# A 31-tap convolution on the tensor engine: from 64-column groups fed by on-chip shifted copies to 32-column groups fed by copies read back from device memory

## The chip, the cores and the metric

The kernel runs on all 8 cores of one Trainium2 chip, one program on each core and no exchange between them. The metric is the device time of the slowest core, in microseconds (us). The runs show two states: in some executions the cores of one die show a lower granted tensor clock and the run is some per cent longer. In one run of the kernel before (1240.1 us) cores 4 to 7 took 1188 to 1239 us at a clock of 0.87 to 0.91, and cores 0 to 3 took 1169 to 1175 us at 0.94 to 0.95. A median with its range is of all runs of a kernel, slow ones too; the ratio to before, with its 95% interval, is of the fast runs alone.

## The reference

One layer of a hybrid decoder trunk is applied to eight prompts of 2048 tokens and 128 short samples of 8 tokens. Each core takes one prompt and 16 samples: 2048 + 128 = 2176 tokens. The part that matters is branch B, a 31-tap depthwise convolution over tokens, per channel:

```python
u = _rmsnorm(h, g_mix)
proj = jnp.einsum('ntd,de->nte', u, w_in)              # D_MODEL = 1024, nine slices of 1024
a_b, a_c, a_h, a_z, b_v, b_g, b_z, gate_a, gate_b = jnp.split(proj, SPLITS, axis=-1)
...
v = b_v * jax.nn.sigmoid(b_g)                          # (N, T, 1024)
ext_b = jnp.concatenate([buf_b.astype(v.dtype), v], axis=1)   # 30 rows of history in front
c = _causal_dwconv(ext_b, w_conv_b) + b_conv_b         # 31 taps, each channel for itself
yb = jax.nn.silu(_layernorm(c, ln_g, ln_b)) * jax.nn.silu(b_z)
...
m = jax.nn.sigmoid(gate_a) * ya + jax.nn.sigmoid(gate_b) * yb
h = h + jnp.einsum('ntd,de->nte', m, w_o)
```

## The kernel before

Tokens are worked off in three blocks (768, 768, and 512 prompt tokens with 128 sample tokens), channels in eight chunks of 128. Operations are not issued as they are written down. They are added to a list (`Sched.add`) with the names of what they read and write, and waits are derived from the names: a read waits for the last writer, a write waits for the last writer and for all readers since.

```python
def add(self, eng, fn, reads=(), writes=(), dma=None):
    ...
    for r in reads:
        w = self.last_writer.get(r)
        if w is not None:
            deps.add(w)
            raw.add(w)
    for r in writes:
        w = self.last_writer.get(r)
        if w is not None:
            deps.add(w)
        for rd in self.readers.get(r, {}).values():
            deps.add(rd)
```

The convolution is a matmul. A group of 64 channels sits on 64 rows of the array, and a copy of it, shifted by one token, on the other 64 rows. So one matmul with a 128x64 diagonal weight does two taps, and 16 of them, each over data shifted by two more tokens, do all taps. Two groups of 64 columns make up a chunk. The shifted copies `R` are made by DMA from on-chip memory to on-chip memory, four loads for each piece of 512, 256 or 128 tokens, into buffers of their own:

```python
for g in range(2):
    for jj in range(2):
        ...
        S.add("sp", lambda e, src=src, dst=dst: e.dma_start(out=dst, in_=src),
              reads=rr, writes=[f"R{rs}_{g}_{jj}"], dma=f"R{rs}_{g}_{jj}")
...
for i in range(16):
    for g in range(2):
        ...
        S.add("pe", lambda e, ...: e.matmul(
            ps[64 * g:64 * g + 64, bc, 0:n], lhsT=Wp[ds][:, 16 * g + i, :], rhs=rhs,
            start=(i == 0), stop=(i == 15), tile_position=(0, 64 * g)), ...)
```

Of the kernel before, what the change touches and what calls it, by code (L numbers as in the profile page):

```python
# [13 lines left out]
KB = 31  # L14
# [5 lines left out]
V_GMIX, V_GPLE, V_BCONV, V_LNG, V_LNB = 0, 8, 16, 24, 32  # L20
V_WCA = 40
V_WCB = 64
V_MASK = V_WCB + 256
NV = V_MASK + 64

BLOCKS = [
    dict(p0=0, npr=768, sbs=[(0, 512, "p"), (512, 256, "p")]),
    dict(p0=768, npr=768, sbs=[(0, 512, "p"), (512, 256, "p")]),
    dict(p0=1536, npr=512, sbs=[(0, 512, "p"), (512, 128, "s")]),
]  # L30

class Sched:
    def __init__(self, nc):
        self.nc = nc
        self.ops = []
        self.last_writer = {}
        self.readers = {}
        self.chan_count = {}

    def add(self, eng, fn, reads=(), writes=(), dma=None):  # L40
        idx = len(self.ops)
        chan = eng if dma is None else ("dma", dma)
        deps = set()
        raw = set()
        for r in reads:
            w = self.last_writer.get(r)
            if w is not None:
                deps.add(w)
                raw.add(w)
# [94 lines left out]

def build_program():
# [9 lines left out]
    p_d = din("p", [NTOK, 256])  # L155
    sa_d = din("sa", [32, D])
    sb_d = din("sb", [480, D])
    w_in = din("w_in", [9 * NCH, 128, D])
    w_oa = din("w_oa", [NCH, 128, D])
    w_ob = din("w_ob", [NCH, 128, D])  # L160
    w_o = din("w_o", [D, D])
# [7 lines left out]
    ncap_d = dout("nca_p", [2, D])  # L169
    ncbp_d = dout("ncb_p", [30, D])  # L170
    ncas_d = dout("nca_s", [32, D])
    ncbs_new_d = dout("ncb_s_new", [128, D])
    ncbs_hist_d = dout("ncb_s_hist", [352, D])

    with contextlib.ExitStack() as st:
# [3 lines left out]
        idf = sb("idf", [128, 128], F32)  # L179
# [5 lines left out]
        histb = sb("histb", [128, NCH, 480], BF16)  # L185
        hista = sb("hista", [128, NCH, 32], F32)
        halo_v = sb("halo_v", [128, NCH, 30], BF16)
# [5 lines left out]
        NRING = 8  # L193
        ring = [sb(f"ring{i}", [128, NCH, 128], BF16) for i in range(NRING)]
# [3 lines left out]
        Wp = [sb(f"Wp{i}", [128, 32, 64], BF16) for i in range(2)]  # L198
        RL = 608
        NRS = 3  # L200
        Rb = [[sb(f"R{i}_{g}", [128, RL], BF16) for g in range(2)] for i in range(NRS)]
        vext = [sb(f"vext{i}", [128, 30 + NTB + 2], BF16) for i in range(2)]
        vexts = [sb(f"vexts{i}", [128, 624], BF16) for i in range(2)]
        sext = [sb(f"sext{i}", [128, 2 + NTB], F32) for i in range(1)]
        sexts = [sb(f"sexts{i}", [128, 160], F32) for i in range(1)]
        xs = [sb(f"xs{i}", [128, D], F32) for i in range(3)]
        xb = [sb(f"xb{i}", [128, D], BF16) for i in range(2)]
        ssq = sb("ssq", [128, 64], F32)
        msq = sb("msq", [128, 64], F32)
        rsd = sb("rsd", [128, 64], F32)  # L210
        NTMP = 6
        tmp = [sb(f"tmp{i}", [128, 512], F32) for i in range(NTMP)]
        accs = sb("accs", [128, NTB], F32)
        accq = sb("accq", [128, NTB], F32)
        rstdB = sb("rstdB", [128, NTB], F32)
        nmrB = sb("nmrB", [128, NTB], F32)
        Abuf = [sb(f"Abuf{i}", [128, D], F32) for i in range(2)]
        Bbuf = sb("Bbuf", [128, D], F32)
        yt = sb("yt", [128, D], F32)
        u2T = sb("u2T", [128, NCH, 128], BF16)  # L220
        pbt = [sb(f"pbt{i}", [128, 256], BF16) for i in range(2)]
        pT = sb("pT", [128, 2, 128], BF16)
        vkeep = sb("vkeep", [128, NCH, 32], F32)
        skeep = sb("skeep", [128, NCH, 2], F32)
        vkeep_s = sb("vkeep_s", [128, NCH, 128], F32)
        BB = [Bbuf[:, :], vkeep_s.rearrange("p a b -> p (a b)")]
        skeep_s = sb("skeep_s", [128, NCH, 32], F32)
# [3 lines left out]
        S = Sched(nc)  # L231

        free_banks = list(range(8))

        def balloc():
            return free_banks.pop(0)

        def bfree(b):
            free_banks.append(b)
# [3 lines left out]
        def talloc():  # L243
            k = tmp_ctr[0] % NTMP
            tmp_ctr[0] += 1
            return k

        ring_ctr = [0]

        SWQ = 4  # L250
        swq_ctr = [0]

        def swq():
            r = f"swq{swq_ctr[0] % SWQ}"
            swq_ctr[0] += 1
            return r

        WL, WG = [], []

        def add_group(srcs):  # L260
            WG.append(list(range(len(WL), len(WL) + len(srcs))))
            for sap in srcs:
                WL.append((sap, len(WG) - 1))
# [4 lines left out]
        for _bi in range(len(BLOCKS)):  # L268
            for j in range(NCH):
                add_group([wcol(4, j), wcol(5, j)])  # L270
            for j in range(NCH):
                add_group([wcol(1, j), wcol(2, j), wcol(0, j), wcol(3, j)])
                if j >= 4:
                    add_group([wcol(6, 2 * (j - 4))])
                    add_group([wcol(6, 2 * (j - 4) + 1)])
            for j in range(NCH):
                add_group([w_oa[j, :, :], w_ob[j, :, :], wcol(7, j), wcol(8, j)])
        wst = dict(nl=0, ng=0, done=set())

        def pump(maxn=4):  # L280
            nem = 0
            while nem < maxn and wst["nl"] < len(WL) and (wst["nl"] < NRING or WL[wst["nl"] - NRING][1] in wst["done"]):
                nem += 1
                t = wst["nl"]
                wst["nl"] += 1
                k = t % NRING
                src = WL[t][0]
                S.add("pool", lambda e, k=k, src=src: e.dma_start(  # L288
                    out=ring[k][:, :, :].rearrange("p k m -> p (k m)"), in_=src),
                    writes=[f"ring{k}", swq()], dma=f"ring{k}")  # L290

        def wgroup():
            g = wst["ng"]
            wst["ng"] += 1
            if not all(t < wst["nl"] for t in WG[g]):
                pump(NRING)
            assert all(t < wst["nl"] for t in WG[g]), "weight tile not prefetched"
            return g, [t % NRING for t in WG[g]]

        def wdone(g):  # L300
            wst["done"].add(g)
            pump()
# [3 lines left out]
        def rms_stats(src_ap, src_res, junk_ap, junk_res):  # L306
            c = stat_ctr[0] % 64
            stat_ctr[0] += 1
            S.add("act", lambda e, c=c: e.activation(out=junk_ap, in_=src_ap, func=AF.Square,
                                                     accum_out=ssq[:, c:c + 1]),  # L310
                  reads=src_res, writes=list(junk_res) + [f"ssq{c}"])
# [9 lines left out]
        def vcol(off, j):  # L321
            return vecs[:, off + j:off + j + 1]

        S.add("sp", lambda e: e.dma_start(out=idf[:], in_=ident_d), writes=["idf"], dma="idf")
        S.add("sp", lambda e: e.dma_start(out=vecs[:], in_=vecs_d), writes=["vecs"], dma="vecs")
        S.add("sp", lambda e: e.dma_start(out=gfin[:], in_=gfin_d), writes=["gfin"], dma="gfin")
        S.add("dve", lambda e: e.tensor_copy(out=idb[:], in_=idf[:]), reads=["idf"], writes=["idb"])
        S.add("pool", lambda e: e.memset(onesf[:], 1.0), writes=["onesf"])
        for i in range(2):
# [119 lines left out]
        for bi, blk in enumerate(BLOCKS):  # L449
# [34 lines left out]
            def s2_proj(j, si):  # L484
                off, n, kind = sbs[si]
                if si == 0:
# [4 lines left out]
                    if j < 2:  # L491
                        diag_build(j)
# [540 lines left out]
```

## Time and profile before

| | before |
|---|---|
| time, median of 3 runs (lowest, highest) | 1180.0 us (1179.0, 1286.6) |
| tensor engine (PE) busy | 1000.9 us, 85% of the span |
| mean granted tensor clock | 0.95 |
| convolution matmuls | 132 us (the two column groups run at once: 32 matmuls of 512 columns in 3.57 us, a pair per 223 ns) |
| waits of the convolution for its copies | 8.7 + 7.5 = about 16 us in all |
| packets on the hardware DMA queue (q1) | 24017, 43.4 MB |

The highest run is slow. PE is TensorE, DVE is VectorE, ACT is ScalarE, SP is the engine whose instruction queue issues the plain DMA loads. "SPq" in a line is that queue at work.

The page of the kernel before says first what is busy (busy us, share of the span, number of instructions):

```profile
PE 1000.9 (85%) x6774; PEld 562.7 (48%) x6774; DVE 560.9 (48%) x927; ACT 356.5 (30%) x661; POOL 231.0 (20%) x512
```

The chain of work that ended last, by engine and by line (a share of the span each):

```profile
PE 64%; DVE 11%; issue 9%; ACT 7%; DMA 7%; SPq 1%; DVEq 0%; POOL 0%; ACTq 0%; POOLq 0%
PE ps L687 13%; PE ps L571 10%; PE ps L790 10%; PE ps L508 9%; PE ps L891 6%; PE ps L779 5%; PE ps L784 5%; PE ps L643 3%; PE ps L844 3%; DMA t_xs<-x 2%; DMA t_R_1<-t_vext 2%; ACT t_tmp L661 2%; DVE t_cbuf L663 2%; DVE t_tmp L653 2%; DVE t_tmp L650 1%
```

The two groups of the convolution, L571, from the costliest groups (busy us, mean ns of one, then idle time just before them and what ended it):

```profile
L571 PE MATMUL ps<-t_R_0,t_Wp 128*64 128x512 bf16 (+2 forms) x768 | 132.5, 326 | 8.7 <-DMA t_R_0<-t_vext 8.7
L571 PE MATMUL ps<-t_R_1,t_Wp 128*64 128x512 bf16 (+2 forms) x768 | 131.7, 326 | 7.5 <-DMA t_R_1<-t_vext 7.5
```

The middle block by stage, from busy time in windows (start:end, length, then busy us and instructions of PE, PEld, DVE, ACT and POOL, then granted clock, DMA share, GB/s): projection with long convolution; short branch, LayerNorm and z gate; output and merge; final token tiles.

```profile
451.00:549.00 98.00, 95.16 (x772) 55.20 (x770) 43.64 (x57) 25.44 (x48) 12.27 (x33) 0.96 0.47 95
549.00:676.00 127.00, 111.34 (x670) 65.09 (x667) 79.94 (x154) 36.35 (x69) 25.94 (x57) 0.96 0.55 85
676.00:758.00 82.00, 81.67 (x498) 49.10 (x499) 26.84 (x50) 17.36 (x34) 16.04 (x31) 0.98 0.59 91
758.00:838.00 80.00, 59.78 (x318) 28.57 (x315) 42.79 (x49) 39.55 (x64) 18.99 (x42) 0.89 0.38 109
```

In the first of them the tensor engine has almost no gap: 95 of 98 us. And the timeline of the SP queue in that stage (start, length, what was issued, how often) shows how the copies are fed: two loads are issued in about 1.1 us.

```profile
469.73 1.19 SPq L542 DMA_DIRECT2D t_R_1<-t_vext  x2
473.60 1.10 SPq L542 DMA_DIRECT2D t_R_0<-t_vext  x2
474.86 1.53 SPq L542 DMA_DIRECT2D t_R_1<-t_vext  x2
```

### The profile page before, as it was taken

The numbers are of one execution on the slowest core, as the hardware profiler recorded it, in microseconds if no ns is written. First come the engines' busy times: TensorE is split into PE (matmuls) and PEld (weight loads), VectorE is DVE, ScalarE is ACT, GpSimd is POOL, SyncE is SP. The second block draws the span as 40 slices with busy tenths as digits, with TensorE's granted clock in tenths as the row PEclk, the third lists the DMA queues.
The fourth block names the chain that finished last, engine by engine and source line by source line (L and its number), as shares of the span: only waits on it lengthen the run. The fifth ranks groups of instructions, "written<-read, shape, count | busy, mean of one in ns | idle before, by whom it ended". The sixth has DMA issues, their size and how long they took to land.

```text
span 1178.2 us, 20798 instructions; the slowest of 8 cores (1166.8 to 1178.2 us)
## 1 busy us (share of the span) xinstructions
PE 1000.9 (85%) x6774; PEld 562.7 (48%) x6774; DVE 560.9 (48%) x927; ACT 356.5 (30%) x661; POOL 231.0 (20%) x512
## 2 busy tenths in 40 slices
PE   1689978988998856999989799987599978789884
PEld 0355645544654423555545465533355544445442
DVE  1334426655333563554566533346555556633353
ACT  3222323233112452223232321245323222332233
POOL 3120102212112121111122121212132222212111
PEclk9899989998999987999998999989799999989997
DMA  9695676554676233546455556633356546576221
GB/s 202 116 155 92 125 165 92 78 84 67 101 107 110 77 127 76 91 90 132 72 90 90 77 77 104 108 94 120 94 108 123 97 76 108 82 152 111 55 79 63
DMA packets 66971, 119.74 MB, mean 102 GB/s; under 512 B 8657, under 2 KB 23377, under 8 KB 66833
## 3 DMA queue, kind: packets, MB, share of 16 engines
q0 software_dynamic: 42848, 75.06, 42.1%
q1 hardware_dynamic: 24017, 43.36, 12.2%
q8 instruction: 56, 0.92, 0.3%
q14 instruction: 50, 0.41, 0.1%
HBM read 172.23 MB, written 11.14 MB: 156 GB/s over the span
## 4 chain that ended last, share of the span: by engine, by line
PE 64%; DVE 11%; issue 9%; ACT 7%; DMA 7%; SPq 1%; DVEq 0%; POOL 0%; ACTq 0%; POOLq 0%
PE ps L687 13%; PE ps L571 10%; PE ps L790 10%; PE ps L508 9%; PE ps L891 6%; PE ps L779 5%; PE ps L784 5%; PE ps L643 3%; PE ps L844 3%; DMA t_xs<-x 2%; DMA t_R_1<-t_vext 2%; ACT t_tmp L661 2%; DVE t_cbuf L663 2%; DVE t_tmp L653 2%; DVE t_tmp L650 1%
## 5 line engine op out<-in xcount | busy, mean ns | idle before, releaser
L687 PE MATMUL ps<-t_uT,t_ring 128*128 128x512 bf16 (+2 forms) x1536 | 254.6, 328 | 40.8 <-ACT t_tmp L661 22.1
L687 PEld LDWEIGHTS ps<-t_uT,t_ring 128*128 128x128 bf16 x1536 | 143.9, 101 | 150.1 <-issue 53.1
L288 POOL DMA_DIRECT2D t_ring<-w_in x216 | 115.7, 536 | 479.4 <-PE ps L508 213.8
L571 PE MATMUL ps<-t_R_0,t_Wp 128*64 128x512 bf16 (+2 forms) x768 | 132.5, 326 | 8.7 <-DMA t_R_0<-t_vext 8.7
L571 PE MATMUL ps<-t_R_1,t_Wp 128*64 128x512 bf16 (+2 forms) x768 | 131.7, 326 | 7.5 <-DMA t_R_1<-t_vext 7.5
L508 PE MATMUL ps<-t_uT,t_ring 128*128 128x512 bf16 (+2 forms) x768 | 130.3, 325 | 0.3 <-DVE t_uT L426 0.3
L790 PE MATMUL ps<-t_uT,t_ring 128*128 128x512 bf16 (+2 forms) x768 | 128.9, 322 | 0.0
L571 PEld LDWEIGHTS ps<-t_R_0,t_Wp 128*64 128x64 bf16 x768 | 75.8, 111 | 53.2 <-issue 21.1
L891 PE MATMUL ps<-t_wpg_t,t_u2T 128*128 128x512 bf16 x272 | 73.5, 432 | 31.5 <-DVE t_u2T L867 22.5
L508 PEld LDWEIGHTS ps<-t_uT,t_ring 128*128 128x128 bf16 x768 | 68.3, 99 | 59.2 <-issue 18.8
L790 PEld LDWEIGHTS ps<-t_uT,t_ring 128*128 128x128 bf16 x768 | 70.9, 99 | 50.5 <-issue 4.4
L801 DVE TENSOR_TENSOR t_tmp<-ps,t_tmp 128x512 f32<-128x512 f32 (+2 forms) x48 | 25.7, 535 | 123.7 <-ACT t_tmp L797 123.7
L571 PEld LDWEIGHTS ps<-t_R_1,t_Wp 128*64 128x64 bf16 x768 | 75.9, 111 | 15.1 <-issue 13.3
L784 PE MATMUL ps<-t_cbuf,t_ring 128*128 128x512 bf16 (+2 forms) x384 | 67.8, 319 | 8.9 <-DVE t_cbuf L663 8.9
L779 PE MATMUL ps<-t_yaT,t_ring 128*128 128x512 bf16 (+2 forms) x384 | 68.5, 322 | 6.3 <-ACT t_tmp L661 4.9
L657 ACT ACTIVATE t_tmp<-t_tmp,t_vecs 128x512 f32<-128x512 f32 (+2 forms) x48 | 33.0, 688 | 121.4 <-DVE t_tmp L653 121.4
L797 ACT ACTIVATE t_tmp<-ps 128x512 f32<-128x512 f32 (+2 forms) x48 | 22.7, 473 | 143.1 <-PE ps L790 142.3
L891 PEld LDWEIGHTS ps<-t_wpg_t,t_u2T 128*128 128x128 bf16 x272 | 28.5, 108 | 74.1 <-issue 52.5
L578 ACT ACTIVATE t_cbuf<-ps,t_vecs 128x512 f32<-128x512 f32 (+2 forms) x48 | 27.0, 563 | 119.6 <-PE ps L571 119.6
L422 PE MATMUL ps<-t_idb,t_xb 128*128 128x128 bf16 x136 | 15.6, 285 | 56.0 <-ACT t_xb L417 56.0
L844 PE MATMUL ps<-t_wo_t,t_cbuf 128*128 128x512 bf16 x272 | 61.0, 379 | 0.0
L643 PE MATMUL ps<-t_uT,t_ring 128*128 128x512 bf16 (+2 forms) x384 | 60.9, 317 | 0.0
(121 smaller groups left out, 1206.0 us busy)
## 6 DMA issues: line engine op xcount, KB each, us to landing
t_ring<-w_in POOLq DMA_DIRECT2D x216, 256.0 KB, 5.6
t_xs<-x SPq DMA_DIRECT2D x34, 512.0 KB, 4.2
y<-t_yt SPq DMA_DIRECT2D x17, 512.0 KB, 2.6
t_ring<-w_oa POOLq DMA_DIRECT2D x24, 256.0 KB, 4.2
t_ring<-w_ob POOLq DMA_DIRECT2D x24, 256.0 KB, 5.3
t_R_0<-t_vext SPq DMA_DIRECT2D x48, 67.8 KB, 2.0
t_R_1<-t_vext SPq DMA_DIRECT2D x48, 67.8 KB, 2.0
t_wo_t<-w_o POOLq DMA_DIRECT2D x2, 1024.0 KB, 10.3
```

The source lines that it names most:

```text
L288: S.add("pool", lambda e, k=k, src=src: e.dma_start(out=ring[k][:, :, :].rearrange("p k m -> p (k m)"), in_=src), writes=[f"ring{k}", swq( ...
L508: S.add("pe", lambda e, b=b, kw=kw, k=k, off=off, n=n: e.matmul(ps[:, b, 0:n], lhsT=ring[kw][:, k, :], rhs=uT[:, k, off:off + n], start=(k ...
L571: S.add("pe", lambda e, bc=bc, ds=ds, i=i, g=g, rhs=rhs, n=n: e.matmul(ps[64 * g:64 * g + 64, bc, 0:n], lhsT=Wp[ds][:, 16 * g + i, :], rhs ...
L578: S.add("act", lambda e, bc=bc, j=j, off=off, n=n: e.activation(out=cbuf[:, j, off:off + n], in_=ps[:, bc, 0:n], func=AF.Identity, bias=vc ...
L643: S.add("pe", lambda e, pz=pz, kz=kz, k=k, off=off, n=n: e.matmul(ps[:, pz, 0:n], lhsT=ring[kz][:, k, :], rhs=uT[:, k, off:off + n], start ...
L657: S.add("act", lambda e, tx=tx, tl=tl, j=j, n=n: e.activation(out=tmp[tl][:, 0:n], in_=tmp[tx][:, 0:n], func=AF.Silu, scale=vcol(V_LNG, j) ...
L687: S.add("pe", lambda e, b=b, kw=kw, k=k, off=off, n=n: e.matmul(ps[:, b, 0:n], lhsT=ring[kw][:, k, :], rhs=uT[:, k, off:off + n], start=(k ...
L779: S.add("pe", lambda e, pya=pya, ka=ka, k=k, off=off, n=n: e.matmul(ps[:, pya, 0:n], lhsT=ring[ka][:, k, :], rhs=yaT[:, k, off:off + n], s ...
L784: S.add("pe", lambda e, pyb=pyb, kbb=kbb, k=k, off=off, n=n: e.matmul(ps[:, pyb, 0:n], lhsT=ring[kbb][:, k, :], rhs=cbufb[:, k, 2 * off:2 ...
L790: S.add("pe", lambda e, b=b, kw=kw, k=k, off=off, n=n: e.matmul(ps[:, b, 0:n], lhsT=ring[kw][:, k, :], rhs=uT[:, k, off:off + n], start=(k ...
L844: S.add("pe", lambda e, h=h, k=k, bm=bm, mcol=mcol: e.matmul(ps[:, bm[h], :], lhsT=cbufb[:, k, mcol:mcol + 128], rhs=wo_t[:, k, 512 * h:51 ...
L891: S.add("pe", lambda e, h=h, k=k, bg=bg: e.matmul(ps[:, bg[h], :], lhsT=u2T[:, k, :], rhs=wpg_t[:, k, 512 * h:512 * h + 512], start=(k == ...
```

## The change

The intent is to cut the tensor work of the convolution further. A matmul now has 32 output columns, and four of them are put side by side on four column groups. On the 128 rows lie 16 channels in eight shifts. For that the tokens are split into even and odd ones (phases), and `v` is written to a scratch in device memory (`vd`), and read back in eight loads of 16 partitions, each shifted by another token: `R[v][16*q : 16*q+16]` is the copy for shift q. In the last block eight more loads fetch the samples' copies from `vs`. The two stages with projections are merged: the short branch of chunk j-1 runs while the copies of chunk j travel. ACT and DVE work on pairs of PSUM banks at once, and there are 14 weight buffers where there were 8.

The copies share on-chip memory with tiles that are used much later, in the final stage of a block (`A0`, `A1`, `B0`, `B1`, `yt`). The scheduler is told by a table `alias`: who writes a name also writes all its aliases. The core of the diff (cuts marked by `...`):

```diff
     def add(self, eng, fn, reads=(), writes=(), dma=None):
...
+        writes = list(writes)
+        for w in list(writes):
+            writes += self.alias.get(w, [])
...
+        reg = sb("reg", [128, 5 * D], F32)
+        regb = reg.bitcast(BF16)
+        Abuf = [reg[:, 0:D], reg[:, D:2 * D]]
+        Bbuf = [reg[:, 2 * D:3 * D], reg[:, 3 * D:4 * D]]
+        yt = reg[:, 4 * D:5 * D]
+        RS = 8 * RW
+        R = [regb[:, RS * i:RS * (i + 1)].rearrange("p (g w) -> p g w", w=RW) for i in range(2)]
...
+        NRD = 16
+        for i, names in enumerate((["A0", "A1", "B0"], ["B0", "B1", "yt"])):
+            for nm in names:
+                S.alias.setdefault(nm, []).extend(f"R{i}_{q}" for q in range(NRD))
+            for q in range(NRD):
+                S.alias[f"R{i}_{q}"] = names
...
-                for g in range(2):
-                    for jj in range(2):
...
-                        S.add("sp", lambda e, src=src, dst=dst: e.dma_start(out=dst, in_=src),
-                              reads=rr, writes=[f"R{rs}_{g}_{jj}"], dma=f"R{rs}_{g}_{jj}")
...
+                S.add("sp", lambda e: e.dma_start(
+                    out=vd[128 * j:128 * j + 128, :, HV + t0:HV + t0 + npr], in_=two(vt[v])[:, :, 0:npr]),
+                    reads=[f"vt{v}"], writes=[f"vd{j}"], dma=f"vd{v}")
...
+                for q in range(8):
+                    ph, s = q // 4, q % 4
+                    S.add("sp", lambda e, q=q, ph=ph, s=s: e.dma_start(
+                        out=R[v][16 * q:16 * q + 16, :, 0:npr + 12],
+                        in_=vd[128 * j:128 * j + 128, ph, t0 + s:t0 + s + npr + 12].rearrange("(g c) w -> c g w", c=16)),
+                        reads=[f"vd{j}", f"vdz{ph}"], writes=[f"R{v}_{q}"], dma=f"R{v}")
...
+                for r in range(2):
+                    for i in range(4):
...
+                            for g in range(4):
...
+                                    ps[32 * g:32 * g + 32, b + r, o0:o1], lhsT=ring[kc][:, wc:wc + 32], rhs=rhs,
...
+                                    tile_position=(0, 32 * g), skip_group_check=True),
...
+            for j in range(1, NCH):
+                s2_proj(j)
+                s3_chunk(j - 1)
+                s2_conv(j - 1)
```

## The prediction

> **What bounds the kernel now.** The tensor engine, with gaps. Page, part 1: PE 85% busy (1000.9 of 1178.2 us), DVE 48%, ACT 30%; the chain of waits is 64% PE. By stage (busy time in windows, middle block, core 4): gate/value projection with long convolution 98 us (PE 95); short branch, LayerNorm and z gate 127 us (PE 111); output/merge 82 us (PE 82); final token tiles 80 us (PE 60, clock 0.89). The second and fourth wait on ACT/DVE chains. DMA is busy about 54%.
>
> **What the change removes.** In the timeline one chunk's projection of 512 tokens is 16 matmuls in 3.56 us. The convolution of those tokens is 32 matmuls in 3.57 us: two 64-column groups run side by side, one pair per 223 ns. A chunk of 768 tokens costs 5.4 us of convolution, about 125 us in all. The new form has 8 rounds of four 32-column groups over 384 columns. [...]this trace shows only the two-group case, plus 27 ns per matmul with its weight load at 128 columns, under the 42 ns needed. Estimate: 8 x 167 ns = 1.4 us a chunk, 4 us saved x 24 = about 90 us, all critical. Also gone: diagonal builds (2.36 us x 24 of DVE, mostly hidden), history and output transposes (about 12 us at 148-161), the p transposes, and the DMA waits of each block's first convolutions (5 us each at 459 and 845, more in the first block).
>
> **What it adds.** 24 weight tiles (each 8 packets per DMA engine of 172 ns: 1.4 us). The v round trip through device memory: per chunk about 0.8 MB in 1024 pieces, at the 48-72 ns measured for 1084 bytes about 3 us per engine. Per chunk of the merged stage DMA needs 7 x 1.4 + 3.5 = 13 us of 17.4 us PE: tight, not bounding. Latency: write, [...]eight issues at 0.55 us, landing: 10-12 us (last block 17-19 us), against 23-28 us until the convolution needs it. Hidden, except perhaps the last chunk. Sigmoid and Silu now alternate: two table loads of 1.28 us per chunk on ACT, hidden.
>
> **Not improved.** The z-gate is a DVE-ACT ping-pong (0.96 x 3 + 0.85 + latencies = 4 us a chunk against 2.6 us PE): about 13 us stall a block. Final tiles stay bound by the ACT/DVE chain: 10.5 us per tile now, I estimate 11 without and 14.5 with next-block normalisation inside: no gain there.
>
> **Sum (us).** Block 0: start 34, merged stage 134+5, LayerNorm/z 36, merge 83, tiles 88 = 380 (was 451). Block 1: 139+36+83+88 = 346 (was 387). Block 2: 122+31+69+65 = 287 (was 340). Total about 1015. Range 965 to 1070; faster by over 2%: 0.95, within 2%: 0.03, slower 0.02.
>
> **What would show it.** Convolution 32 matmuls in 1.3-1.8 us; merged stage 17-18 us a chunk with PE over 95%; waits of the convolution for R small; PE busy about 86-88%; DMA share about 70%; final tiles 11-15 us each with PE about 60%.
>
> **What would make it wrong.** The four groups not overlapping (up to +60 us); R arriving late because it shares DMA engines with 14 prefetched weight tiles, or the SP queue (19 issues a chunk in the last block) falling behind; a granted clock lowered by denser PE work; final tiles much better or worse than the hand count.

The blocks' 380 + 346 + 287 us make 1013, given as about 1015. The 1.4 us for a chunk's convolution, and with it the saving of about 90 us, took it that four groups overlap fully. The trace of before shows that for two (a pair of 512 columns per 223 ns, so 167 ns for 384); the step to four was the estimate, and e1 measured it later (44 ns a matmul). The latency of 10 to 12 us isn't in the sum, since it was taken as hidden. Of its parts, before shows a store of `y` that lands in 2.6 us, an issue in 0.55 us and a copy that lands in 2.0 us: 2.6 + 8 x 0.55 + 2.0 = 9.0 us, and 13.4 us with the last block's 16 issues, where 17 to 19 were predicted. The rest wasn't shown.

Two statements of the text can be set beside the traces. A table load on ACT took 1.28 us in before and in after, and after has 42 of them (L492 and L642) for its 24 chunks, where two a chunk were predicted. And a clock lowered by denser tensor work was a risk, not something a trace of before shows: in e1's middle block 72 us of tensor work without a gap ran at a granted clock of 1.00.

## The result, and the profile after

| | before | after |
|---|---|---|
| time, median of 4 runs | 1179.5 us | 1583.0 us (1581.8 to 1585.5) |
| ratio of the fast runs, with its 95% interval | | 1.343 (1.340 to 1.345) |
| PE busy | 1000.9 us, 85% | 934.1 us, 59% |
| mean granted tensor clock | 0.95 | 0.80 |
| waits of the convolution for its copies | about 16 us | 494 us |
| packets on the hardware DMA queue (q1) | 24017, 43.4 MB | 58784, 55.8 MB |

A ratio here is the mean time of one kernel's fast runs over the mean of the other's fast runs of the same rounds. So it isn't quite the ratio of the medians quoted beside it. The prediction was 1015 us, range 965 to 1070: it was wrong, and in direction too.

Busy time and granted clock of the page of after (the second line has one digit for each fortieth of the span, in tenths of full speed):

```profile
PE 934.1 (59%) x6156; PEld 544.9 (34%) x6156; DVE 504.7 (32%) x643; ACT 359.5 (23%) x448; POOL 215.9 (14%) x468
PEclk8777778599988779878689989866776676588998
```

The chain that ended last is no longer tensor work. It is DMA, and most of that the copies read back from `vd`:

```profile
DMA 55%; PE 21%; DVE 9%; ACT 7%; issue 5%; POOL 2%; SPq 1%; DVEq 0%; ACTq 0%; POOLq 0%
DMA t_reg<-vd 39%; PE ps L452 16%; DMA t_reg<-vs 8%; DMA vd<-t_vt 5%; ACT t_junk L330 3%; DMA t_xs<-x 2%; PE ps L731 2%; ACT t_tmp L694 2%; DVE t_tmp L692 1%; DVE t_cbuf L697 1%; PE ps L764 1%; DVE t_tmp L689 1%; DVE t_reg L737 1%; DVE t_reg L780 1%; DVE t_reg L782 1%
```

The convolution's group, L541 now, answers to the two L571 lines of before. Its work fell to 62.6 us, and 494 us of idle time stand before it:

```profile
L541 PE MATMUL ps<-t_reg,t_ring 128*32 128x384 bf16 (+2 forms) x1024 | 62.6, 426 | 494.1 <-DMA t_reg<-vs 257.5
```

The merged stage of the three blocks, from busy time in windows (columns as before). They were predicted at 139, 139 and 122 us. Note the DMA share, the last but one column: 0.64, 0.51, 0.37. The DMA engines have time to spare.

```profile
51.00:323.00 272.00, 147.42 (x976) 82.51 (x977) 74.51 (x103) 51.97 (x60) 38.48 (x74) 0.75 0.64 111
545.00:805.00 260.00, 147.91 (x1000) 83.83 (x999) 79.15 (x107) 54.06 (x63) 34.93 (x71) 0.80 0.51 87
1018.00:1400.00 382.00, 124.53 (x1232) 86.86 (x1231) 74.73 (x145) 48.61 (x61) 33.88 (x82) 0.66 0.37 66
```

The timeline of the tensor engine in the middle block shows the rhythm. 16 us of projections follow on 2.75 us of convolution, then comes a wait of 12 us for a copy; one chunk takes 31 us.

```profile
707.69 2.75 PE L541 MATMUL ps<-t_reg,t_ring 128*32 128x384 bf16 x32 [12.35 <-DMA t_reg<-vd]
710.37 16.11 PE L452 MATMUL ps<-t_uT,t_ring 128*128 128x384 bf16 x96
739.01 2.75 PE L541 MATMUL ps<-t_reg,t_ring 128*32 128x384 bf16 x32 [12.52 <-DMA t_reg<-vd]
```

A wait for a copy may mean that the copy travelled slowly, or that it set out late. The timeline of the SP queue tells these apart. The eight loads of one chunk took 24.9 us and 29.4 us to *issue*, where two loads of before took 1.1 us:

```profile
616.24 24.92 SPq L510 DMA_DIRECT2D t_reg<-vd  x8
641.26 0.52 SPq L501 DMA_DIRECT2D vd<-t_vt  x1
644.41 29.39 SPq L510 DMA_DIRECT2D t_reg<-vd  x8
673.89 0.52 SPq L501 DMA_DIRECT2D vd<-t_vt  x1
```

What SP waited for in between (total us, times, longest), whole run:

```profile
SPq L135 <- DMA t_reg<-vd: 568.1, 179, 8.6
...
SPq L135 <- DMA t_reg<-vs: 108.8, 58, 2.5
```

SP waits for its own loads, 237 times and 677 us long. The chain of waits in that stretch (start, length, what) is those loads, one behind the other:

```profile
644.41 2.72 DMA t_reg<-vd
...
647.19 4.50 DMA t_reg<-vd
...
651.75 6.27 DMA t_reg<-vd
```

Nothing in the data asks for this. The eight loads of a chunk write eight different stripes of partitions. But each is named a writer of `A0`, `A1` and `B0` (or `B0`, `B1`, `yt`) by the alias table, and so each is a second writer of what the load before it wrote. The rule "a write waits for the last writer" then makes SP wait until the load before has landed. The dependency that was wanted, that the first copy of a block mustn't overwrite a final tile still in use, needs only the first load of a block into each of the two buffers to wait.

### The profile page after: what moved, and what is told of

It reads as the page before. It is cut to its first block, busy times and chain, and to the rows that moved or that the text cites. A ratio compares the mean times of both kernels' runs of the same rounds, so it can differ in the third digit from the quotient of the medians.

```text
span 1583.8 us, 17598 instructions; the slowest of 8 cores (1555.1 to 1583.8 us)
## 1 busy us (share of the span) xinstructions
PE 934.1 (59%) x6156; PEld 544.9 (34%) x6156; DVE 504.7 (32%) x643; ACT 359.5 (23%) x448; POOL 215.9 (14%) x468
## 2 busy tenths in 40 slices
DMA packets 105750, 139.25 MB, mean 88 GB/s; under 512 B 16832, under 2 KB 59840, under 8 KB 105664
## 3 DMA queue, kind: packets, MB, share of 16 engines
q1 hardware_dynamic: 58784, 55.76, 13.1%
## 4 chain that ended last, share of the span: by engine, by line
DMA 55%; PE 21%; DVE 9%; ACT 7%; issue 5%; POOL 2%; SPq 1%; DVEq 0%; ACTq 0%; POOLq 0%
DMA t_reg<-vd 39%; PE ps L452 16%; DMA t_reg<-vs 8%; DMA vd<-t_vt 5%; ACT t_junk L330 3%; DMA t_xs<-x 2%; PE ps L731 2%; ACT t_tmp L694 2%; DVE t_tmp L692 1%; DVE t_cbuf L697 1%; PE ps L764 1%; DVE t_tmp L689 1%; DVE t_reg L737 1%; DVE t_reg L780 1%; DVE t_reg L782 1%
## 5 line engine op out<-in xcount | busy, mean ns | idle before, releaser
L452 PE MATMUL ps<-t_uT,t_ring 128*128 128x384 bf16 (+1 forms) x3456 | 569.1, 326 | 20.2 <-ACT t_tmp L686 17.0
L452 PEld LDWEIGHTS ps<-t_uT,t_ring 128*128 128x128 bf16 x3456 | 344.1, 100 | 241.6 <-issue 52.2
L541 PE MATMUL ps<-t_reg,t_ring 128*32 128x384 bf16 (+2 forms) x1024 | 62.6, 426 | 494.1 <-DMA t_reg<-vs 257.5
L541 PEld LDWEIGHTS ps<-t_reg,t_ring 128*32 128x32 bf16 x1024 | 34.5, 137 | 518.0 <-issue 502.9
L714 DVE TENSOR_TENSOR t_tmp<-ps,t_tmp 128x768 f32<-128x768 f32 (+1 forms) x48 | 43.8, 914 | 156.3 <-PE ps L452 152.8
L705 ACT ACTIVATE t_tmp<-ps 128x768 f32<-128x768 f32 (+1 forms) x48 | 36.9, 775 | 176.1 <-PE ps L452 176.1
L452 PE MATMUL ps<-t_cbuf,t_ring 128*128 128x384 bf16 (+1 forms) x384 | 67.4, 330 | 12.9 <-DVE t_cbuf L697 8.8
L452 PE MATMUL ps<-t_yaT,t_ring 128*128 128x384 bf16 (+1 forms) x384 | 62.9, 317 | 3.7 <-ACT t_tmp L686 3.7
L495 DVE TENSOR_TENSOR t_vt<-ps,t_tmp 128x768 bf16<-128x768 f32 (+1 forms) x24 | 21.9, 913 | 97.3 <-ACT t_tmp L492 67.1
L452 PEld LDWEIGHTS ps<-t_cbuf,t_ring 128*128 128x128 bf16 x384 | 38.4, 101 | 37.6 <-issue 17.1
L645 DVE TENSOR_TENSOR t_tmp<-ps,t_tmp 128x768 f32<-128x768 f32 (+1 forms) x24 | 21.9, 913 | 87.4 <-PE ps L452 83.7
```

The lines of the kernel that those rows point to most:

```text
L452: S.add("pe", lambda e, b=b, k_=k_, k=k, rhs=rhs, si=si: e.matmul(ps[:, b + si, 0:n], lhsT=ring[k_][:, 128 * k:128 * k + 128], rhs=rhs(k, si),
L495: S.add("dve", lambda e: e.tensor_tensor(out=two(vt[v]), in0=pp(bv), in1=two(tg), op=ALU.mult), reads=pres(bv) + [tgr], writes=[f"vt{v}"])
L541: S.add("pe", lambda e, b=b, r=r, i=i, g=g, wc=wc, rhs=rhs, o0=o0, o1=o1, part=part: e.matmul(ps[32 * g:32 * g + 32, b + r, o0:o1], lhsT=r ...
L705: S.add("act", lambda e: e.activation(out=two(tg), in_=pp(bg), func=AF.Sigmoid), reads=pres(bg), writes=[tgr, tgr + "o"])
L714: S.add("dve", lambda e: e.tensor_tensor(out=two(tg), in0=pp(b), in1=two(tg), op=ALU.mult), reads=pres(b) + [tgr], writes=[tgr])
```

## The experiments

All experiments are edits of the kernel after, except one. They ran in four groups on three chips (e1 to e3; e4 to e7; e8 to e10; e11 and e12 on the same chip as those), each group beside runs of the kernel before; therefore ratios to before are compared across groups, and 1% of ratio is about 12 us. The texts of expectation give theories letters. The main theory (A) is the one above: a chain of loads that wait for one another. Its rivals are that the way through device memory is slow by itself, and that the DMA engines are overloaded by bytes or by many small pieces.

### e1_no_chain: the loads of a chunk don't wait for one another

```diff
-    def add(self, eng, fn, reads=(), writes=(), dma=None):
+    def add(self, eng, fn, reads=(), writes=(), dma=None, after=None):
...
-        for w in list(writes):
-            writes += self.alias.get(w, [])
+        if after is None:
+            for w in list(writes):
+                writes += self.alias.get(w, [])
...
+        for r in after or ():
+            deps.add(self.last_writer.get(r))
+            deps.update(self.readers.get(r, {}).values())
+        deps.discard(None)
...
-                        reads=[f"vd{j}", f"vdz{ph}"], writes=[f"R{v}_{q}"], dma=f"R{v}")
+                        reads=[f"vd{j}", f"vdz{ph}"], writes=[f"R{v}_{q}"], dma=f"R{v}",
+                        after=S.alias[f"R{v}_0"] if q == 0 else [])
```

The first load of a chunk still waits for the last users of the shared memory, and every load still waits for the write of `v`. That last wait follows from the data, since the loads read what the write puts into `vd`; no run here left it out. The convolution waits for all loads of its chunk. The edit drops one more wait: by the shared `B0`, the first load of a chunk waited for the last of the chunk before. In the trace above that one was hidden, since the first load goes out only when the write of `v` has landed (641.26 + 3.04 us).

> The kernel after, with one thing undone: the eight (last block sixteen) loads of one chunk's shifted copies no longer wait for one another; the first still waits for the buffers it shares memory with. Theory A (the loads were chained one after another by the bookkeeping of the shared memory, and this chain of 28-30 us a chunk, 45-50 in the last block, is what the merged stage runs at): the stage falls from about 30 and 47 us a chunk to 17-19 us, the total to 1015-1080 us, the granted clock back to 0.93-0.96, and waits of the convolution for its copies from 494 us to under 40. Rival B (the way through device memory in pieces of 0.5-0.8 KB is itself too slow, or shares the DMA engines badly with the weights): the loads of a chunk still need over 25 us together and the total stays above 1400 us. Rival C (the dense tensor work is throttled): the clock stays near 0.80.

Measured: correct; 1195.5 us (1179.9 to 1208.7), ratio to before 1.003 (0.985 to 1.021), against 1.343 for the kernel after. The chain cost 0.34 x 1179 = about 400 us, give or take 20. The convolution's group and a stretch of the chain of waits in the middle block:

```profile
L548 PE MATMUL ps<-t_reg,t_ring 128*32 128x384 bf16 (+2 forms) x1024 | 48.6, 355 | 105.9 <-DMA t_reg<-vd 53.8
```

```profile
518.17 1.41 PE ps L548 x32
519.58 15.71 PE ps L457 x96
535.29 1.41 PE ps L548 x32
```

Waits fell from 494 to 106 us, and in the middle block a chunk takes 15.71 + 1.41 = 17.1 us without a gap, the very rhythm that was predicted (17.4). The 32 convolution matmuls take 1.41 us at a granted clock of 1.00 (518 to 590 us, core 4). In the kernel after they took 2.75 us, always after a wait (8.6 to 39.6 us on the slowest core), and the clock granted meanwhile was 0.50 (707.69 to 710.37 us; 0.98 in the projections that follow). In the last block's timelines of e1 (core 4), e8 (core 5) and e10 (core 2), the 64 convolution matmuls of a chunk took 1.29 or 1.30 us after no wait for a copy or one of up to 3.19 us, and 2.32 or 2.33 us after each wait of 3.87 to 14.91 us. The border isn't that sharp everywhere: in e1's block 0 the 32 matmuls took 2.65 us after a wait of 2.37 us. What slows them wasn't tested.

Rival B as it was stated (total above 1400 us) falls with the total, though sharing the DMA engines comes back below on a smaller scale. Rival C falls with the clock: with the same tensor work it rose from 0.80 to between 0.88 and 0.91, so the low clock had followed from the waits (0.93 to 0.96 had been expected).

But the whole is no faster than before, and 1195 us is above the range expected. What remained shows in the windows of the first and the last block's merged stage (e1_no_chain, core 0): 184 and 165 us instead of 139 and 122, at a DMA share of 0.97 and 0.88.

```profile
52.00:236.00 184.00, 137.48 (x967) 78.56 (x966) 74.24 (x103) 51.85 (x60) 38.79 (x74) 0.89 0.97 160
828.00:993.00 165.00, 119.40 (x1247) 84.56 (x1245) 76.44 (x149) 49.07 (x63) 35.57 (x85) 0.88 0.88 151
```

So with the chain gone a second cause comes up: in these two stages the DMA engines are nearly full. Cores differ by some us in a stage. So where one run's last merged stage is compared with another's below, the figure is the median of the cores, from the block's first projection to the LayerNorm sums: 171 us in e1.

### e2_half_chain: every second link only

```diff
-                        after=S.alias[f"R{v}_0"] if q == 0 else [])
+                        after=S.alias[f"R{v}_0"] if q == 0 else [f"R{v}_{k}" for k in range(q - 2, q) if q % 2 == 0])
...
-                            after=[])
+                            after=[f"R{v}_{k}" for k in range(8 + q - 2, 8 + q) if q % 2 == 0])
```

Loads go out in pairs, and a pair waits for the pair before. The bytes, the pieces and the way through device memory are the same as in e1 and in after; only the number of links differs.

> As e1_no_chain, but the loads go in pairs and each pair waits for the pair before: half as many links. Theory A: a chunk costs about 3.5 us for the write and 4 x 3.8 us, 19 us, in the first two blocks (hardly over the 17.5 us of the tensor engine) and about 31 us in the last; total some 130-160 us above e1_no_chain, about 1200 us. Rival B: the same time as e1_no_chain within 2%.

Measured: correct; 1358.6 us (1356.9 to 1361.0), ratio 1.148 (1.138 to 1.158). Counting the waits between loads of one chunk: after has 7 in each of 16 chunks and 15 in each of 8, which is 232; e2 has 3 and 7, which is 104; e1 has none. From e1 to e2 the ratio rises by 0.145, which is 171 us or 1.6 us a link. From e1 to after it rises by 0.340, which is 400 us or 1.7 us a link. The time goes with the number of links, at one price a link. That is what theory A asks, and slow memory or full engines can't give it, since they are the same in all three. (The total of about 1200 us was missed because e1 itself had been expected at 1015 to 1080 us; the distance from e1, 171 us, is a little over the 130 to 160 expected.)

### e3_before_chained: the kernel before with such a chain

```diff
-                              reads=rr, writes=[f"R{rs}_{g}_{jj}"], dma=f"R{rs}_{g}_{jj}")
+                              reads=rr, writes=[f"R{rs}_{g}_{jj}", "rchain"], dma=f"R{rs}_{g}_{jj}")
```

One extra name makes each of the old kernel's 192 on-chip copies a second writer of the same thing. No byte goes through device memory.

> The kernel before, with its four loads of shifted copies per job (SBUF to SBUF, no device memory) put in one chain through an added false resource. Theory A: each load of 2 us to landing plus issue becomes one link of about 2.4 us, so a chunk of two jobs takes about 19 us against 10.9 us of tensor work, in 24 chunks: total 1320-1380 us. Rival B (device memory is the cause): within 3% of the kernel before.

Measured: correct; 1413.2 us (1408.6 to 1459.2), ratio 1.195 (1.182 to 1.208). This is more than expected, 230 us for 191 links, or 1.2 us a link. In the chain that ended last tensor work gives way to DMA (PE from 64% to 40%, DMA from 7% to 35%), as in the kernel after:

```profile
PE 40%; DMA 35%; DVE 10%; issue 8%; ACT 6%; SPq 1%; DVEq 0%; POOL 0%; ACTq 0%; POOLq 0%
```

So the chain alone ruins a kernel without any of the change's other parts. What sets the price of a link (1.2 us here, 1.7 there) was not separated. It may be the part of a load's landing time that isn't hidden under tensor work; no run tests that.

### e4_zeros_apart: the history zeros on another queue

In e1 the first block starts late. Its fifth tile of x is 20 us late, since two small writes of zeros to `vd`, each of 1024 pieces of 30 bytes, stand before it in the same queue. A view of four microseconds of the DMA queues of e1 (packets, MB, share of 16 engines):

```profile
q0 software_dynamic: 272, 0.50, 99.9%
q1 hardware_dynamic: 270, 0.01, 8.6%
```

q0 carries weights in pieces of 2048 bytes, q1 the zeros. In these four microseconds both got nearly the same number of pieces through, 270 and 272. So here the queue of tiny pieces moved at about one tiny piece for each large one of the other queue. In what order the engines take them isn't shown.

```diff
-            S.add("sp", lambda e, ph=ph: e.dma_start(
+            S.add("act", lambda e, ph=ph: e.dma_start(
                 out=vd[:, ph, 0:HV].rearrange("(j p) h -> p j h", p=128), in_=zt[:, :, ph, :]),
-                reads=["zt"], writes=[f"vdz{ph}"], dma="vdz")
+                reads=["zt"], writes=[f"vdz{ph}"], dma=f"vdz{ph}")
```

> e1_no_chain, with the two writes of zero history (2048 pieces of 30 bytes) issued from the scalar engine's queue instead of the queue of the x loads. Theory D (on each DMA engine the small pieces of one queue alternate one for one with the 2 KB pieces of the weight queue while weights are waiting: in e1 295 pieces of 30 B beside 294 weight pieces in 4 us, so 128 pieces an engine hold the queue for 27 us and the fifth x tile lands at 43.6 us): that x tile lands before 25 us, the second half of the first projection starts at 30-36 us instead of 52, total 12-20 us below e1_no_chain (ratio to before about 0.985-0.995 against 1.003). Rival E (the DMA engines are simply full of 14 weight tiles at the start): start moves by under 5 us.

Measured: correct; 1181.4 us (1180.3 to 1204.4), ratio 0.997 (0.989 to 1.005). The statistics of the fifth x tile start at 23.85 us where e1 had 43.68, so the cause of the late start is right:

```profile
23.85 1.06 ACT L335 ACTIVATE t_junk<-t_xs 128x1024 bf16<-128x1024 f32 x1 [2.27 <-DMA t_xs<-x]
```

But the intervals of e4 and e1 overlap, so a gain in time isn't shown. What the start won, the stage behind it lost again: block 0's merged stage ended at 235 us in e1 and at 231 us in e4 (median of the cores), so 4 of the 20 us were left. That it lost them because DMA is still short there is an argument; no run took it apart.

### e5_late_resident: large resident weights loaded one stage later

```diff
-                if bi == 0 and j - 1 < len(RESIDENT):
-                    RESIDENT[j - 1]()
...
+                if bi == 0 and j < len(RESIDENT):
+                    RESIDENT[j]()
```

This is e1 with the loads of `w_o`, `w_pg` and `w_pe` moved from block 0's merged stage to its output stage. Bytes and pieces stay the same; only the time changes at which they compete with the copies.

> e1_no_chain, with the loads of the weights that stay (w_o, w_pg, w_pe: 18 tiles' worth) moved from the merged stage of block 0 to its output stage. Theory D: without this backlog the small loads of block 0 wait less; its merged stage falls from about 185 us to 150-160, total 20-35 us below e1_no_chain (ratio to before about 0.975-0.985). Block 2 unchanged at about 172 us. Rival F (the loads of block 0 are late for another reason, such as the latency of device memory): the stage stays above 175 us.

Measured: correct; three of five runs were slow, and the two fast ones took 1153.5 and 1161.9 us, ratio 0.977 (0.966 to 0.988), as expected. Block 0's merged stage ended at 204 us where e1 had 235 (median of the cores), from the same start at about 52 us: some 150 us, as expected, and rival F falls. In time it is 0.020 of ratio or 23 us below e4, which ran in the same rounds and differs from e1 only by the zeros. So when the same bytes are asked for matters: part of e1's excess was these loads in block 0.

### e6_long_pieces: one long piece per partition

The scratch is laid out so that a partition of a load is one run of 4.3 to 6.4 KB, where it was eight runs of 0.5 to 0.8 KB. The channels are permuted on the host, and the history halo is kept on chip, which also does away with the zeros. The core of the edit to e1:

```diff
-                        out=R[v][16 * q:16 * q + 16, :, 0:npr + 12],
-                        in_=vd[128 * j:128 * j + 128, ph, t0 + s:t0 + s + npr + 12].rearrange("(g c) w -> c g w", c=16)),
-                        reads=[f"vd{j}", f"vdz{ph}"], writes=[f"R{v}_{q}"], dma=f"R{v}",
+                        out=R[v][16 * q:16 * q + 16, 0:8 * wb - 3],
+                        in_=vd[j, ph, s:s + 128 * wb].rearrange("(c x) -> c x", c=16)[:, 0:8 * wb - 3]),
+                        reads=[f"vd{j}"], writes=[f"R{v}_{q}"], dma=f"R{v}",
```

> e1_no_chain, with the scratch laid out so that each partition of a load is one run of 4.3-6.4 KB instead of eight of 0.5-0.8 KB (same bytes within 1%, an eighth of the pieces), the history kept in SBUF, so no zero writes either. Theory D: the loads of a chunk land in under 4 us, waits of the convolution fall from 106 us to under 25 us; merged stage about 150 us in block 0, 142 in block 1, 125 in block 2, start as in e4_zeros_apart; total 1085-1120 us (ratio 0.92-0.95). Rival G (bytes, not pieces, load the engines): block 2's merged stage stays above 155 us and total above 1150 us.

Measured: correct; 1157.1 us (1154.2 to 1176.4), ratio 0.977 (0.966 to 0.987). Packets of all queues fell from 105750 to 74998, those of the hardware queue from 58784 to 28032, but the gain fell short of what was expected. In block 0 single chunks came down to 17.1 us, the later ones took up to 25 (core 0). And the last block's merged stage hardly moved, 170 us after e1's 171, and its DMA share stayed (core 0, a slower core than the median):

```profile
800.00:975.00 175.00, 124.78 (x1252) 87.19 (x1251) 77.17 (x157) 49.57 (x63) 34.73 (x85) 0.83 0.86 147
```

So in the last block it wasn't the size of the copies' pieces that held them up. The expectation that these pieces were the main remaining cause fell here, and rival G (stage above 155 us, total above 1150) stands.

### e7_long_late: e6 and e5 together

The edit is the one of e5, made to e6.

> e6_long_pieces and e5_late_resident together. Theory D: pieces are so few that the backlog of block 0 matters little, so 5-20 us below e6_long_pieces: 1070-1110 us (ratio 0.91-0.945). It should be the fastest so far and beat the kernel before by 5-9%.

Measured: correct; 1137.8 us (1134.7 to 1147.5), ratio 0.962 (0.954 to 0.970): less gain than expected, though the first version over 2% faster than the kernel before with its whole interval. Its last merged stage takes 169 us (median of the cores) against 122 predicted.

### e8_four_loads: half as many loads, the same bytes

```diff
-                for q in range(8):
...
-                        out=R[v][16 * q:16 * q + 16, 0:8 * wb - 3],
...
+                for s in range(4):
+                    S.add("sp", lambda e, s=s: e.dma_start(
+                        out=R[v][32 * s:32 * s + 32, 0:8 * wb - 3],
+                        in_=bass.AP(tensor=vb.tensor, offset=vb.offset + s, ap=[[8 * wb, 32], [1, 8 * wb - 3]])),
```

Both phases go in one load of 32 partitions: four loads a chunk, eight in the last block. This tests whether the number of loads or SP's issue time bounds the rest.

> e7_long_late with half the load instructions: four loads of 32 partitions per chunk (eight in the last block) in place of eight of 16 (sixteen); same pieces, same bytes. Theory H (what is left of the loss in the last block is the in-order SP queue: per chunk 11 us until the write has landed, 16 issues of 0.54 us, other issues, together about 21 us against 15 us of tensor work): 4.3 us less a chunk, the merged stage of block 2 falls from about 170 us to 135-145, blocks 0 and 1 change by under 10 us; total 1095-1115 us (ratio to before 0.93-0.95). Rival D alone (the DMA engines' alternation with weights sets it, issues do not matter): within 1% of e7_long_late.

Measured: correct; 1130.6 us (1129.9 to 1138.5), ratio 0.961 (0.958 to 0.965), the same as e7 in ratio. The last merged stage went from 169 to 163 us (median of the cores), not to the 135 to 145 expected, and the run as a whole hardly moved. The number of loads is not what is left.

### e9_fewer_pieces: other small transfers out of the way

```diff
+            if last:
+                S.add("sp", lambda e: e.dma_start(out=vk_d.rearrange("(j p) t w -> p j t w", p=128), in_=vkeep[:]),
+                      reads=[f"vkeep{j}" for j in range(NCH)], dma="vk")
...
-                if bi == 0 and j == 7:
-                    sample_history()
...
+                if bi == 1 and j == 5:
+                    sample_history()
```

The kept rows of `v` are stored once at the end of the stage and no longer per chunk, and the samples' history is set up in block 1.

> e8_four_loads, with two more sets of small pieces taken out of the merged stage: the outputs of v (256 pieces of 316 B per chunk of the last block) are kept in SBUF and stored once later, and the sample history (2048 pieces of 480 B with cast, 2048 of 704 B) is loaded and stored in block 1's output stage instead of block 0's merged stage. Theory D: the write of v no longer queues behind the 316-byte pieces: its landing in block 2 falls from 11 us to 7-9, the last convolution of block 0 comes about 8-10 us sooner; total 10-25 us below e8_four_loads. Rival: under 5 us.

Measured: correct; median 1138.0 us, but three of five runs, the profiled one among them, were slow. The two fast ones took 1117.0 and 1127.3 us, ratio 0.953 (0.947 to 0.959). That is about 10 us below e8 by ratio, but on only two runs, and the intervals overlap. The traces show the effect where it was expected: in the last merged stage the write of `v` landed in a median of 8.2 to 8.5 us on the undisturbed die (cores 0 to 3), where e8 had 10.7 to 12.9 on the same cores, and the stage took 157 us there after 160.

### e10_late_conv: the last convolution of a block behind other work

```diff
-            s2_conv(7)
-            s3_chunk(7, mid=ln_stats)
+            s3_chunk(7, mid=lambda: s2_conv(7), end=ln_stats)
```

The last convolution of a block has no next chunk to hide its copies behind. Here it comes after the first two projections of the last short-branch chunk.

> e9_fewer_pieces, with the last convolution of each block moved behind two projections of the last short-branch chunk (5 us of tensor work) and the LayerNorm sums behind the other two. If the waits for the last chunk's copies (3-9 us a block before) are what costs there, 5-20 us below e9_fewer_pieces; if the LayerNorm chain behind it simply starts later, no gain (within 0.5%).

Measured: correct; 1113.5 us (1111.8 to 1125.3), ratio 0.945 (0.943 to 0.947). This is the best version found: 5.5% faster than the kernel before. What this step alone brought isn't shown: the interval touches e9's, and the last merged stage stayed at 158 us (median of the cores). Its busy time and its convolution group (core 2):

```profile
PE 906.9 (82%) x6156; PEld 533.0 (48%) x6156; DVE 507.6 (46%) x683; ACT 357.8 (32%) x448; POOL 218.5 (20%) x468
```

```profile
L551 PE MATMUL ps<-t_reg,t_ring 128*32 128x384 bf16 (+2 forms) x1024 | 41.3, 318 | 56.3 <-DMA t_reg<-vs 31.7
```

The convolution takes 41.3 us, against 132 before: 91 us of tensor work less, where 90 were predicted. The three merged stages on that core, the slowest:

```profile
33.00:181.00 148.00, 135.54 (x987) 78.37 (x985) 76.84 (x119) 51.51 (x61) 35.82 (x69) 0.96 0.99 168
403.00:553.00 150.00, 137.84 (x1010) 80.24 (x1009) 80.15 (x123) 52.77 (x63) 36.02 (x71) 0.97 0.94 157
769.00:930.00 161.00, 122.00 (x1260) 85.28 (x1259) 76.69 (x158) 48.70 (x63) 35.24 (x86) 0.88 0.93 162
```

### e11_fewer_weights: a wrong result

To see whether weights and copies compete in the last block's merged stage, 24 of the 56 weight tiles that belong to it aren't loaded; the matmuls use whatever the buffers hold. The result is wrong.

```diff
+                m = t - SKIP0[0]
+                if 2 <= m < 56 and m % 7 in (4, 5, 6):
+                    continue
```

> e10_late_conv, wrong on purpose: in the merged stage of the last block 24 of the 56 weight tiles are not loaded (the ring keeps older weights there), the instructions of every engine but those loads unchanged. Result wrong for the last block only. Theory J (in the last block the DMA engines, shared by weights and copies, set the stage: 96% busy, v's write needs 8.5 us to land instead of 3): 33 us less weight traffic, the stage falls from 161 us to 125-140 us, the write lands in under 6 us, total 20-35 us below e10_late_conv (about 1080-1092). Rival K (the latency of the round trip and the in-order SP queue set it whatever the weights do): stage above 152 us, total within 10 us.

Measured: three of five runs were slow; the two fast ones took 1096.6 and 1100.9 us, ratio 0.930 (0.922 to 0.938). That is 14 us (by the mean of the fast runs) to 17 us (by ratio) below e10: the direction expected, and less than the 20 to 35 us. The profiled run is slow, but the die of cores 0 to 3 in it was undisturbed, so its core 1 is compared with core 2 of e10. The last merged stage shrank from 161 to 145 us, so rival K (above 152 us) falls. Core 2 is e10's slowest, so the pair flatters the effect: by the median of the cores it went from 158 to 147 us.

```profile
763.00:908.00 145.00, 117.59 (x1265) 83.28 (x1263) 76.73 (x159) 48.71 (x63) 25.85 (x68) 0.93 0.78 147
```

The write of `v`, which the copies must wait for, landed in a median of 8.5 us in e10 (first line) and of 2.6 us in e11 (second fence; the columns are loads, KB each, median us to landing):

```profile
vd<-t_vt SPq DMA_DIRECT2D x7, 135.5 KB, 8.5
```

```profile
vd<-t_vt SPq DMA_DIRECT2D x7, 135.5 KB, 2.6
```

In e10 the convolutions of this stage waited for copies 14.9, 0.6, 3.9, 1.7 and 10.7 us, 32 us in all. In e11 the waits in the middle are gone; the first (9.3 us) and the last (9.0 us) remain. So the weights' loads in the DMA engines caused the waits in the middle and a part of the first and the last. The rest of these two may be the way of a copy itself, with nothing in front of it to hide it; no run took it apart. And where waits for copies went, another grew a little: that of the projection for DVE's second read of a PSUM pair (the kept rows of `v`), from 7.3 to 9.1 us. The expectation took none of this into account.

### e12_chain_again: the best version with the chain put back

```diff
-                        after=S.alias[f"R{v}_0"] if s == 0 else [])
+                        after=S.alias[f"R{v}_0"] if s == 0 else [f"R{v}_{s - 1}"])
...
-                            reads=[f"vs{j}", "vsh"], writes=[f"R{v}_{4 + s}"], dma=f"R{v}", after=[])
+                            reads=[f"vs{j}", "vsh"], writes=[f"R{v}_{4 + s}"], dma=f"R{v}", after=[f"R{v}_{3 + s}"])
```

> e10_late_conv with the chain put back: each of the four (last block eight) loads of a chunk waits for the one before. From the three earlier points (256 links in the kernel after: 1583 us; 128 in e2_half_chain: 1359; none within a chunk in e1_no_chain: 1180-1196) a link costs 1.6-1.8 us on average; here 4 x 16 + 8 x 8 = 128 links, of which the first of each chunk is there anyway: about 104 x 1.7 = 175 us more: 1270-1310 us (ratio to before 1.07-1.11). If the layout with long pieces had removed the cost of waiting one after another, it would stay below 1160 us.

Measured: correct; 1270.7 us (1257.4 to 1277.3), ratio 1.072 (1.063 to 1.081), as expected. 0.127 of ratio is 150 us for 104 links, 1.4 us a link. The SP queue in the middle block shows the chain again: four loads of a chunk take 11.90 us to issue (first line, e12, core 7), and 1.71 us in e10 (second line, core 2):

```profile
566.44 11.90 SPq L518 DMA_DIRECT2D t_reg<-vd  x4
450.26 1.71 SPq L518 DMA_DIRECT2D t_reg<-vd  x4
```

Long pieces, few loads and a tidier DMA schedule don't take the price of the chain away.

## Why the prediction was wrong

The prediction was 1015 us and the measurement 1583 us: 568 us apart. The runs split this as follows, with ratios times 1179 us:

| step | from | to | difference |
|---|---|---|---|
| loads of a chunk chained | 1583 (after) | about 1183 (e1) | about 400, give or take 20 |
| DMA order and pieces, late convolution | about 1183 (e1) | 1114 (e10) | about 70, give or take 20 |
| not recovered | 1114 (e10) | 1015 | 99 |

**The step that failed: "Latency: write, [...] eight issues at 0.55 us, landing: 10-12 us (last block 17-19 us), against 23-28 us until the convolution needs it. Hidden".** The prediction took the eight loads as independent, one issue after the other, and so as a latency. In the trace the eight issues took 25 to 29 us instead of 4.4, since each waits for the load before to land. That is no latency that a slack of 23 to 28 us could hide. SP handles chunk after chunk in order, so 3 us for the write and 25 to 29 us for the loads are the period of a chunk (28 to 33 us; about 45 us in the last block, by the convolutions at 1077.5, 1123.5 and 1168.7), against 17 us of tensor work. The cause stood in the diff, in three lines of the scheduler and a table of names; it was read as a matter of memory and not as a wait. The warning in the prediction, "the SP queue (19 issues a chunk in the last block) falling behind", named the right queue for the wrong reason: the number of issues costs little (e8: half as many loads, and the last merged stage went from 169 to 163 us), the waits between them cost 400 us. e1, e2, e3 and e12 show this four ways.

**A term mis-sized: "DMA needs 7 x 1.4 + 3.5 = 13 us of 17.4 us PE: tight, not bounding".** Without the chain, the DMA engines are full or nearly so in the merged stage of block 0 and of the last block (shares 0.97 and 0.88 in e1, 0.99 and 0.93 in e10). Even where no copy was late, in e1's middle block (core 4), the share was 0.98:

```profile
518.00:590.00 72.00, 72.00 (x559) 42.26 (x558) 43.56 (x61) 29.10 (x34) 20.72 (x39) 1.00 0.98 166
```

That is 16.8 us of DMA in a chunk of 17.1 us, where the term had 13. By queue, the weights took 71.6% of that stretch, 12.3 us a chunk instead of 7 x 1.4 = 9.8, and the copies with the rest of the hardware queue 26.4%, 4.5 us instead of 3.5. For the weights the prediction's "8 packets per DMA engine of 172 ns" took a median for a mean: in the DMA records of before (core 4) a weight piece of 2048 bytes takes 173 ns in the median and 213 ns in the mean, and in e1 222 ns in the mean. Counting a whole chunk's bytes against the chunk's time also left out the resident weights of block 0 (e5: about 23 us) and the zeros in front of the x tiles (e4: 20 us at the start, 4 of them at the end of the stage), and took no account of the copies waiting for their turn beside the weights: in e10 the write of `v` landed in 8.5 us instead of 2.6. The prediction had listed "R arriving late because it shares DMA engines with 14 prefetched weight tiles" as a risk. It was real, but it came to tens of us, not hundreds.

**Right: the convolution.** "8 x 167 ns = 1.4 us a chunk": 1.41 us measured at a granted clock of 1.00. Its share of tensor time fell by 91 us (132 to 41.3 in e10), and 90 were predicted. That this agrees to 1 us is partly luck: both terms came out about 7 us above the prediction's (125, and 24 x 1.4 = 34). The four groups do run side by side: in e1's middle block 32 matmuls in 1.41 us are 44 ns each, where the projection's 96 of the same 384 columns, in 15.71 us, are 164 ns each. **Right: the merged stage at 17 to 18 us a chunk** wherever the copies are there: 17.1 us in e1's middle block.

**Right: no gain in the final tiles.** 95 and 89 us in e10, against 88 predicted and 80 in the middle block of before. **Right in e10, not in after: "DMA share about 70%"** (51.7% and 18.5% on the two queues of e10). The agreement is partly luck: 0.70 of e10's 1112 us is about 70 us more of DMA time than 0.70 of the 1015 predicted.

The 99 us not recovered, by stage, hand count against e10 (core 2):

| us | start | merged | LayerNorm/z, merge | tiles |
|---|---|---|---|---|
| block 0, predicted / e10 | 34 / 33 | 139 / 148 | 119 / 127 | 88 / 95 |
| block 1 | | 139 / 150 | 119 / 127 | 88 / 89 |
| block 2 | | 122 / 161 | 100 / 110 | 65 / 72 |

In the first two merged stages the convolution waits only twice, for the first copies (8.3 and 7.9 us) and for the last (4.2 and 4.3 us): 12 us each, where the prediction allowed 5 (its "134+5"), so 7 of the excess of 9 and 11 us. Its allowance was for the last chunk alone ("except perhaps the last chunk"); the first chunk's copies, with no earlier chunk's work to hide them, it overlooked. In the last block 32 us of such waits and 7 us of waits for DVE stand against an excess of 39 us. e11 bears this out for the part that the weights' loads cause. The 1 to 10 us in each of the other stages are hand estimates that were a few per cent low. No experiment took them apart, so their causes stay open, as does the price of a link, which lay between 1.2 and 1.7 us.

## What to carry to other kernels

When buffers are overlaid in one memory, look at what the dependency tracker makes of it: several partial writes to disjoint parts, each declared a writer of the shared name, become a chain in which every DMA waits for the one before to land (here 232 links and about 400 us). The queue that took 25 us to issue eight loads wasn't slow but waiting for itself, and the timeline of the issuing queue and the list of what it waits for (677 us for its own loads) show this at once, while the DMA share falls (0.37 in the last merged stage of after, 0.88 in e1). Before calling a latency hidden, ask whether the queue that carries it handles the next round in order: then its duration is a period to be compared with the round's work, and slack doesn't help.
